# Weight blocks 129 columns apart, and four starting offsets for the chunks, in a float32r kernel of two layers

## The chip, the cores and the metric

The kernel runs on one core of a Trainium2 chip. The metric is the device time of one execution in microseconds (us). The engines are called as in the profile: PE is TensorE's matmul side and PEld its weight loads, DVE is VectorE, ACT is ScalarE, POOL is GpSimd, and SP issues most of the DMAs.

## The reference, cut to what matters

Two transformer layers follow each other on 256 tokens of width 1024 (the first adds 16 meta tokens, so that part of it works on 272 columns). Nearly all of the arithmetic is a chain of products of activations with weight matrices:

```python
# first layer
h = h + 0.5 * swiglu(rms_norm(h, ffn1_norm), ffn1_w_in, ffn1_w_out)   # 1024 -> 2 x 2816 -> 1024
h = h + token_mixer(rms_norm(h, mix_norm), ...)                       # w_in, two attentions, two branches, w_out
h = h + 0.5 * swiglu(rms_norm(h, ffn2_norm), ffn2_w_in, ffn2_w_out)
# second layer
h = h + head_group_mixer(rmsnorm(h), ...)                             # convolution and retention
h = h + memory_cross_attention(rmsnorm(h), rmsnorm(mem), ...)
h = h + jnp.square(jax.nn.relu(rmsnorm(h) @ up_w)) @ down_w           # 1024 -> 4096 -> 1024
```

All inputs and outputs are float32.

## The kernel before

Activations are held with the features on the 128 partitions and the tokens along the free axis: `XH[:, k]` is feature block k of the normed input for 256 tokens (272 in the first feed-forward network and the key and value projections). Each float32 operand is split into a float32r high part and a float32r low part that holds the rest, and each product is made of three float32r matmuls (`mm3`, lines 512 to 515): high weights by high activations, high weights by low activations, low weights by high activations. In each of them the weight block, 128 by 128, is the stationary operand (a weight load of its own, shown as PEld) and the activations are the moving operand, 256 or 272 columns. In `products_t` (lines 1005 to 1007) it is the other way round: 512 weight columns move past a stationary block of activations.

The weights come from HBM as chunks of at most 2048 columns, in the order of use (`_plan`). A chunk is a row of blocks, and nearly all blocks are 128 columns wide; 8 blocks of the forget gate have 8 columns, and the blocks for `products_t` have 512. `_Weights` handles a chunk in three steps, and each kind of tile has three buffers:

- `load` brings the chunk to a tile `raw` (SP's queue);
- `_high` (line 319, ACT) copies up to 1024 columns of `raw` to `hi`, which rounds them to float32r;
- `piece` (line 335, DVE) writes `lo = raw - hi` for the same columns.

`get(key)` gives PE the columns of `hi` and `lo` that hold one block. `core.step` sets the order: it first splits what the step's matmuls need, lets PE run, and splits for later steps, up to 4096 columns ahead, between the pieces of the work that empties PSUM. Everything is in the order in which the program writes it; no scheduler moves anything.

Where things lie in a partition matters for the change. A `hi` or `lo` tile is 2112 columns (8448 bytes, 33 times 256) wide, and its blocks begin 16 columns in:

```python
t = self.pool.tile([P, CH + LINE], F32R, tag=tag, bufs=3, name=f"{tag}{c}")   # CH = 2048, LINE = 64
return t[:, SHIFT : SHIFT + CH]                                               # SHIFT = 16
```

By the addresses that the program is given, every 128-column weight block of the kernel before begins 192 bytes past a multiple of 256, and every moving activation operand 128 bytes past one. The feature blocks of XH and XL lie 320 columns apart (1280 bytes). Some projections read their 256 moving columns as two runs of 128 that lie 144 columns (576 bytes) apart (`xq`); the second run then begins 192 bytes past a multiple of 256, as the weights do.

Three further places serve as measures below. The eight blocks of 8 columns (`fa`) begin 32 bytes further each. In the attention heads three float32 transposes (lines 688 to 690) load a block of the softmax result as weights; the third begins 144 columns (576 bytes) into the tile in the first eight heads and 145 columns (580 bytes) in the other eight. And line 814 (`factor`) is a DVE product whose operands are two runs of 128 columns.

Of the kernel before, what the change touches and what calls it, by code (L numbers as in the profile page):

```python
# [10 lines left out]
F32 = mybir.dt.float32  # L11
F32R = mybir.dt.float32r
I32 = mybir.dt.int32
AF = mybir.ActivationFunctionType
ALU = mybir.AluOpType
AX = mybir.AxisListType

P = 128
# [5 lines left out]
TP = 288  # L24
XP = 320
LINE = 64
SHIFT = 16
DFF = 2816
MF = DFF // P
DFF2 = 4096  # L30
# [4 lines left out]
CH = 2048  # L35
# [239 lines left out]
class _Weights:  # L275
# [2 lines left out]

    def __init__(self, nc, pool, ws):
        self.nc, self.pool, self.ws = nc, pool, ws  # L280
        _, self.where, self.start, self.ends, self.total = _plan()
        self.raw, self.hi, self.lo = {}, {}, {}
        self.loaded = 0
        self.c, self.o = 0, 0
        self.begun = []
        self.done = 0
        self.used = 0
        self.free = 0
        self.beside = None
# [16 lines left out]
    def _part(self, tag, c):  # L306


        t = self.pool.tile([P, CH + LINE], F32R, tag=tag, bufs=3, name=f"{tag}{c}")
        return t[:, SHIFT : SHIFT + CH]  # L310

    def _high(self, n):
        c, a = self.c, self.o
        at, size = self.start[c]
        if a == 0:
            self.hi[c] = self._part("hi", c)
            self.lo[c] = self._part("lo", c)
        b = min(a + n, size)
        self.nc.scalar.activation(self.hi[c][:, a:b], self.raw[c][:, a:b], AF.Copy)  # L319
        self.begun.append((c, a, b))  # L320
        self.c, self.o = (c + 1, 0) if b == size else (c, b)

    def piece(self, to, n=1024):


        if to is None or self.done >= to or self.done >= self.total:
            return False
        while sum(self.start[self.free]) <= self.used:
            self.free += 1
        while len(self.begun) < 2 and self.c < min(len(self.start), self.free + 3):  # L330
            self._high(n)
        c, a, b = self.begun.pop(0)
        if self.beside:
            self.beside((b - a) / 1024)
        self.nc.vector.tensor_tensor(self.lo[c][:, a:b], self.raw[c][:, a:b], self.hi[c][:, a:b].bitcast(F32),  # L335
                                     op=ALU.subtract)
        self.done = self.start[c][0] + b
        if b == self.start[c][1]:
            self.load()
        return True  # L340
# [16 lines left out]
    def get(self, key):  # L357
        c, off, n = self.where[key]
        self.used = max(self.used, self.start[c][0] + off + n)
        return self.hi[c][:, off : off + n], self.lo[c][:, off : off + n]  # L360


# [1243 lines left out]
```

## Time and profile before

| what | value |
|---|---|
| median of 2 runs | 983.17 us (982.59 to 983.75) |
| the profiled execution | 983.64 us |
| its span, from the first to the last instruction | 981.6 us |
| PE busy | 965.1 us (98% of the span), 7667 matmuls |
| DVE busy | 675.4 us (69%) |
| ACT busy | 537.5 us (55%) |
| DMA moved | 169.05 MB, 172 GB/s on average |

Matmuls are pipelined: one takes some 0.28 us from start to end, and the next starts before it has ended, so a PE that is "busy" may still be waiting in part. What a matmul costs is read from the distance between the starts of two matmuls, called the spacing here. In a table of stretches, the spacing is the stretch plus 0.28 us (the matmuls that had begun before it are counted) divided by the count of matmuls.

### The profile page before, as it was taken

How to read it: one execution, taken by the hardware profiler on the slowest of the kernel's cores; microseconds unless marked ns; L12 is line 12 of the kernel's file. 1: busy time of each engine (PE TensorE's matmuls, PEld its weight loads, DVE VectorE, ACT ScalarE, POOL GpSimd, SP SyncE). 2: the span in 40 equal slices, each digit the busy share in tenths (PEclk: the TensorE clock that was granted, in tenths of full speed). 3: DMA queues.
4: the chain of work that ended last, by engine and by line, in shares of the span. 5: the costliest groups of instructions: out<-in, count | busy, mean ns of one | idle time of the engine just before them, and what ended most of it. 6: DMA issues, size and time to landing. Idle time of an engine off the chain costs nothing.

```text
span 981.6 us, 18397 instructions
## 1 busy us (share of the span) xinstructions
PE 965.1 (98%) x7667; PEld 935.2 (95%) x7667; DVE 675.4 (69%) x1232; ACT 537.5 (55%) x927; POOL 9.9 (1%) x15
## 2 busy tenths in 40 slices
PE   7999999999999999999999999999999999999996
PEld 7999999999989899999999999889899999999996
DVE  5686656657875758677666657999976677675552
ACT  6545444456574656666454447556484566554441
POOL 0000000020000000000000000000000000000000
PEclk9999999999999999999999999999999999999999
DMA  8674526554523225554544656443544256555431
GB/s 298 191 264 172 173 92 233 191 185 138 173 94 123 96 99 214 215 215 173 194 166 157 209 191 235 168 155 138 202 159 155 86 182 221 199 194 194 173 128 43
DMA packets 31363, 169.05 MB, mean 172 GB/s; under 512 B 5144, under 2 KB 8864, under 8 KB 14640
## 3 DMA queue, kind: packets, MB, share of 16 engines
q1 hardware_dynamic: 30928, 167.34, 48.3%
q8 instruction: 60, 0.98, 0.4%
q10 hardware_dynamic: 288, 0.52, 0.1%
q14 instruction: 23, 0.19, 0.1%
q0 software_dynamic: 64, 0.01, 0.0%
HBM read 166.79 MB, written 1.07 MB: 171 GB/s over the span
## 4 chain that ended last, share of the span: by engine, by line
PE 75%; ACT 1%; DVE 1%; issue 0%; DVEq 0%
PE ps L513 14%; PE ps L515 14%; PE ps L514 14%; PE po L515 7%; PE po L514 7%; PE po L513 7%; PE ps L660 1%; PE ps L1007 1%; PE ps L1006 1%; PE ps L1005 1%; PE po L702 1%; PE ps L1308 1%; PE ps L1174 0%; PE po L1346 0%; PE po L716 0%; PE ps L766 0%
## 5 line engine op out<-in xcount | busy, mean ns | idle before, releaser
L335 DVE TENSOR_TENSOR lo<-raw,hi 128x1024 fp32r<-128x1024 f32 (+2 forms) x334 | 373.4, 1130 | 47.5 <-ACT hi L319 45.0
L319 ACT ACTIVATE hi<-raw 128x1024 fp32r<-128x1024 f32 (+2 forms) x334 | 321.8, 978 | 137.2 <-issue 43.8
L513 PE MATMUL ps<-XH,hi 128*128 128x256 f32 (+2 forms) x976 | 284.0, 291 | 5.7 <-ACT hi L319 4.3
L515 PE MATMUL ps<-XH,lo 128*128 128x256 f32 (+2 forms) x976 | 277.4, 284 | 0.8 <-DVE lo L335 0.8
L514 PE MATMUL ps<-XL,hi 128*128 128x256 f32 (+2 forms) x976 | 277.6, 284 | 0.0
L513 PEld LDWEIGHTS ps<-XH,hi 128*128 128x128 f32 (+1 forms) x976 | 184.4, 189 | 8.2 <-ACT hi L319 4.3
L514 PEld LDWEIGHTS ps<-XL,hi 128*128 128x128 f32 (+1 forms) x976 | 186.0, 191 | 1.8 <-DVE XL L527 0.5
L515 PEld LDWEIGHTS ps<-XH,lo 128*128 128x128 f32 (+1 forms) x976 | 184.3, 189 | 1.4 <-DVE lo L335 1.0
L513 PE MATMUL po<-XH,hi 128*128 128x256 f32 (+1 forms) x456 | 130.2, 285 | 0.2 <-DVE br L1071 0.2
L515 PE MATMUL po<-XH,lo 128*128 128x256 f32 (+1 forms) x456 | 129.0, 283 | 0.4 <-DVE lo L335 0.4
L514 PE MATMUL po<-XL,hi 128*128 128x256 f32 (+1 forms) x456 | 128.7, 282 | 0.0
L514 PEld LDWEIGHTS po<-XL,hi 128*128 128x128 f32 x456 | 86.7, 190 | 0.1
L515 PEld LDWEIGHTS po<-XH,lo 128*128 128x128 f32 x456 | 85.8, 188 | 0.6 <-DVE lo L335 0.6
L513 PEld LDWEIGHTS po<-XH,hi 128*128 128x128 f32 x456 | 85.7, 188 | 0.6 <-DVE br L1071 0.5
L624 ACT ACTIVATE s<-gr 128x272 f32<-128x272 f32 (+1 forms) x44 | 18.7, 426 | 108.5 <-DVE gr L622 108.5
L513 PE MATMUL ps<-AHf,hi 128*128 128x272 f32 (+1 forms) x220 | 62.4, 284 | 0.0
L514 PE MATMUL ps<-ALf,hi 128*128 128x272 f32 (+1 forms) x220 | 62.4, 284 | 0.0
L515 PE MATMUL ps<-AHf,lo 128*128 128x272 f32 (+1 forms) x220 | 62.4, 284 | 0.0
L1045 DVE SCALAR_TENSOR_TENSOR cv<-U,par,cv 128x256 f32<-128x256 f32 x120 | 50.1, 479 | 0.2 <-ACT cv L1078 0.2
L622 DVE TENSOR_TENSOR gr<-ps,r 128x272 f32<-128x272 f32 (+1 forms) x28 | 12.1, 434 | 48.4 <-PE ps L515 42.1
L513 PE MATMUL ps<-AHm,hi 128*128 128x256 f32 x160 | 45.0, 281 | 0.0
L514 PE MATMUL ps<-ALm,hi 128*128 128x256 f32 x160 | 45.0, 281 | 0.0
(385 smaller groups left out, 1827.8 us busy)
## 6 DMA issues: line engine op xcount, KB each, us to landing
raw<-in_ws_dram SPq DMA_DIRECT2D x128, 1024.0 KB, 4.8
raw<-in_ws_dram SPq DMA_DIRECT2D x32, 704.0 KB, 4.2
raw<-in_ws_dram SPq DMA_DIRECT2D x3, 512.0 KB, 5.6
dec<-in_dec_dram SPq DMA_DIRECT2D x1, 1536.0 KB, 6.4
BM<-drow SPq DMA_DIRECT2D x2, 512.0 KB, 5.7
memraw<-in_mt_dram SPq DMA_DIRECT2D x1, 1024.0 KB, 7.0
hA<-in_xt_dram SPq DMA_DIRECT2D x3, 273.0 KB, 6.0
raw<-in_ws_dram SPq DMA_DIRECT2D x3, 256.0 KB, 6.7
```

The costliest lines, as they stand in the source:

```text
L319: self.nc.scalar.activation(self.hi[c][:, a:b], self.raw[c][:, a:b], AF.Copy)
L335: self.nc.vector.tensor_tensor(self.lo[c][:, a:b], self.raw[c][:, a:b], self.hi[c][:, a:b].bitcast(F32), op=ALU.subtract)
L513: T.matmul(o, w[0], x[0], start=start, stop=False)
L514: T.matmul(o, w[0], x[1], start=False, stop=False)
L515: T.matmul(o, w[1], x[0], start=False, stop=stop)
L622: V.tensor_tensor(gr, g[:, :n], r[0][:, :n], op=ALU.mult)
L624: S.activation(s, gr, AF.Silu)
L660: T.matmul(ps[:, at : at + n], lhs, rhs, start=True, stop=True)
L702: T.matmul(o, st["v"](h, 0), pt[:, :SEQ], start=t % 2 == 0, stop=False)
L1005: T.matmul(ps[i], xh[:, t], wh, start=k == 0, stop=False)
L1006: T.matmul(ps[i], xl[:, t], wh, start=False, stop=False)
L1045: V.scalar_tensor_tensor(cv[:, m], U[:, m, j : j + SEQ], prm("cw", m * 31 + j), cv[:, m], op0=ALU.mult, op1=ALU.add)
```

## The change

In the split parts `hi` and `lo`, blocks of 128 columns now begin 129 columns (516 bytes) apart, with one unused column behind each. `raw` stays as it was. `_high` and `piece` therefore write (and `piece` reads `hi`) as runs of 128 with a step of 129: a piece of 1024 columns has the shape 8 x 128. Chunks with blocks of other widths (the one with the 8-column blocks, and those of `products_t`) keep blocks that touch. The fixed `SHIFT` of 16 columns gives way to a start of `16 * (c % 4)` columns for chunk c, and a tile is 16 columns wider (8512 bytes, 33.25 times 256), so the three buffers themselves begin 64 bytes further each, modulo 256. The six tiles take 384 bytes more in all, and what is allocated behind them moves by that: the moving operands there (AHf, AHm, OFH, OS, OXH, CH and their low parts, and YL) begin at a multiple of 256 bytes instead of 128 past one; XH, XL, YH, MH and ML stay.

No instruction is added, removed or moved on any engine. The start of a weight block now takes each of the 64 possible places of a 4-byte word in 256 bytes, with 86 to 142 matmuls each.

```diff
-SHIFT = 16
+GAP = 1
...
-        _, self.where, self.start, self.ends, self.total = _plan()
+        self.chunks, self.where, self.start, self.ends, self.total = _plan()
...
-        t = self.pool.tile([P, CH + LINE], F32R, tag=tag, bufs=3, name=f"{tag}{c}")
-        return t[:, SHIFT : SHIFT + CH]
+        t = self.pool.tile([P, CH + 16 + LINE], F32R, tag=tag, bufs=3, name=f"{tag}{c}")
+        at = 16 * (c % 4)
+        return t[:, at : at + CH + 16]
+
+    def _gap(self, c):
+        return GAP if all(b[4] == P for b in self.chunks[c]) else 0
+
+    def _blocks(self, t, c, a, b):
+
+        w = P + self._gap(c)
+        i, j = a // P, b // P
+        if w == P or a % P or b % P:
+            return t[:, a:b]
+        return t[:, i * w : j * w].rearrange("p (i w) -> p i w", w=w)[:, :, :P]
+
+    def _plain(self, t, c, a, b):
+        if not self._gap(c):
+            return t[:, a:b]
+        return t[:, a:b].rearrange("p (i w) -> p i w", w=P)
...
-        self.nc.scalar.activation(self.hi[c][:, a:b], self.raw[c][:, a:b], AF.Copy)
+        self.nc.scalar.activation(self._blocks(self.hi[c], c, a, b), self._plain(self.raw[c], c, a, b), AF.Copy)
...
-        self.nc.vector.tensor_tensor(self.lo[c][:, a:b], self.raw[c][:, a:b], self.hi[c][:, a:b].bitcast(F32),
-                                     op=ALU.subtract)
+        self.nc.vector.tensor_tensor(self._blocks(self.lo[c], c, a, b), self._plain(self.raw[c], c, a, b),
+                                     self._blocks(self.hi[c], c, a, b).bitcast(F32), op=ALU.subtract)
...
         self.used = max(self.used, self.start[c][0] + off + n)
+        off += off // P * self._gap(c)
         return self.hi[c][:, off : off + n], self.lo[c][:, off : off + n]
```

## Rows read from the trace of the kernel before

**Rows 1.** The page, part 1: busy time and share of each engine.
```profile
PE 965.1 (98%) x7667; PEld 935.2 (95%) x7667; DVE 675.4 (69%) x1232; ACT 537.5 (55%) x927; POOL 9.9 (1%) x15
```

**Rows 2.** Stretches, PE alone: us, busy (matmuls), granted clock, DMA share, GB/s.
```profile
35.00:205.00 170.00, 170.00 (x1381) 1.00 0.56 189
...
362.00:410.00 48.00, 48.00 (x426) 1.00 0.60 216
415.00:588.00 173.00, 173.00 (x1471) 1.00 0.53 184
602.00:613.00 11.00, 11.00 (x100) 1.00 0.35 111
...
723.00:737.00 14.00, 14.00 (x126) 1.00 0.59 204
775.00:798.00 23.00, 23.00 (x205) 1.00 0.48 162
805.00:965.00 160.00, 160.00 (x1361) 1.00 0.48 172
```

**Rows 3.** PE in order of time, 410.5 to 412.0 us: start, duration, instruction.
```profile
410.52 0.28 PE L515 MATMUL ps<-XH,lo 128*128 128x256 f32 x1
410.64 0.28 PE L513 MATMUL ps<-XH,hi 128*128 128x256 f32 x1
...
410.86 0.28 PE L515 MATMUL ps<-XH,lo 128*128 128x256 f32 x1
410.98 0.59 PE L562 MATMUL ps<-acc,c 128*128 128x256 f32 x2
411.22 0.47 PE L513 MATMUL po<-XH,hi 128*128 128x256 f32 x1
411.53 0.28 PE L514 MATMUL po<-XL,hi 128*128 128x256 f32 x1
411.65 0.28 PE L515 MATMUL po<-XH,lo 128*128 128x256 f32 x1
411.76 0.28 PE L513 MATMUL po<-XH,hi 128*128 128x256 f32 x1
```

**Rows 4.** PE in order of time, the forget gate's blocks of 8 columns.
```profile
237.32 0.29 PE L514 MATMUL ps<-XL,hi 128*8 128x272 f32 x1
...
237.82 0.28 PE L515 MATMUL ps<-XH,lo 128*8 128x272 f32 x1
237.94 0.29 PE L513 MATMUL ps<-XH,hi 128*8 128x272 f32 x1
...
238.31 0.29 PE L513 MATMUL ps<-XH,hi 128*8 128x272 f32 x1
238.44 0.29 PE L514 MATMUL ps<-XL,hi 128*8 128x272 f32 x1
...
240.05 0.29 PE L515 MATMUL ps<-XH,lo 128*8 128x272 f32 x1
```

**Rows 5.** PE in order of time, moving operand of two runs 576 bytes apart.
```profile
316.20 0.28 PE L513 MATMUL ps<-XH,hi 128*128 128x256 f32 x1
...
316.92 0.28 PE L513 MATMUL ps<-XH,hi 128*128 128x256 f32 x1
```

**Rows 6.** PE in order of time, transposes of a head of the second attention.
```profile
348.75 0.27 PE L688 MATMUL ps<-cst,p 128*128 128x128 f32 x1
348.86 0.27 PE L689 MATMUL ps<-cst,p 128*128 128x128 f32 x1
348.97 0.27 PE L690 MATMUL ps<-cst,p 128*128 128x128 f32 x1
```

**Rows 7.** All instructions of line 690: duration in ns, shortest, median, longest.
```profile
L690 PEld LDWEIGHTS ps<-cst,p x16: 138/140/144, 271.5 to 348.9; 128*128 128x128 f32 x16
```

**Rows 8.** Groups by line and shape on DVE: busy us, mean ns, idle before.
```profile
L335 DVE TENSOR_TENSOR lo<-raw,hi 128x1024 fp32r<-128x1024 f32 x291 | 352.6, 1219 | 47.2 <-ACT hi L319 44.7
...
L1414 DVE TENSOR_TENSOR a<-ps,t 128x256 f32<-128x256 f32 x20 | 8.4, 422 | 0.9 <-ACT t L1412 0.8
...
L814 DVE TENSOR_TENSOR hB<-ps,r 128x256 f32<-128x256 f32 x8 | 3.4, 424 | 7.1 <-PE ps L515 7.1
```

**Rows 9.** Groups by line and shape in 615 to 704 us, DVE.
```profile
L335 DVE TENSOR_TENSOR lo<-raw,hi 128x1024 fp32r<-128x1024 f32 x26 | 31.7, 1219 | 0.0
```

**Rows 10.** Stretch 615 to 704 us: us, then PE, PEld, DVE, ACT, POOL busy, clock, DMA.
```profile
615.00:704.00 89.00, 88.85 (x581) 78.61 (x581) 87.27 (x168) 48.19 (x74) 0.00 (x0) 1.00 0.43 155
```

**Rows 11.** Waits: who waited for whom, us in total, times, longest us.
```profile
DVE lo L335 <- ACT hi L319: 45.0, 34, 2.5
```

## Prediction

> **What bounds the kernel now.** I read the shares first: PE is busy for 965.1 us of the 981.6, its weight loads for 935.2, DVE for 69% and ACT for 55% [rows 1]. So PE sets the time, and the question is what one matmul costs. That is the spacing of starts, and the table of stretches gives it, at a granted clock of 1.00 throughout, which is the 2.4 GHz level [rows 2]. In the first feed-forward network, 272 columns wide: (170 + 0.28) / 1381 = 123.3 ns. In the second, 256 columns wide: 173.28 / 1471 = 117.8 ns, and in the last one 160.28 / 1361 = 117.8 ns. But in four other stretches with the same shape of matmul it is 48.28 / 426 = 113.3 ns, 112.8, 113.3 and 113.6 ns [rows 2]. Columns alone would take 256 / 2.4 = 106.7 ns and 272 / 2.4 = 113.3 ns. So 6.7 to 11 ns go astray in each matmul, and for one shape there are two levels of loss.
>
> The rows in order of time show where a level changes. Up to 410.86 us the matmuls start 0.11 us apart, then a statistic of two float32 passes (line 562) comes between, and behind it they start 0.12 us apart and stay so [rows 3]; the next such stretch holds for 173 us. DVE's work and the DMAs change all the time meanwhile, the spacing does not: it is a rhythm into which matmul and weight load fall, and which lasts until something interrupts it. In the kernel before, every weight block and every moving operand stand in the same relation modulo 256 bytes, so nothing in the addresses can push the rhythm out again. The change gives each block another relation.
>
> **The change part by part.** *Split pieces on DVE.* The same 334 instructions, with runs of 128 instead of one run. A DVE product of 256 columns takes 422 ns in one run and 424 ns in two [rows 8]; seven more runs in a piece of 1024 are then 14 ns on 1219. Between 615 and 704 us DVE is busy for 87.27 of 89 us, and there it can set the pace [rows 10]; 26 such pieces fall there [rows 9]: 26 x 14 ns = 0.4 us. Elsewhere DVE's idle time covers it. I take 0. *Copies on ACT.* No pair of rows compares one run with eight. DVE waited 45 us for these copies, in 34 waits [rows 11], but the splits run ahead of PE, and at 14 ns each as on DVE it would be under 0.5 us on 34 of them; I take 0 as well.
>
> *Weight loads from an address that is no multiple of 64 bytes.* The trace has such loads: of the 16 loads at line 690 eight begin 4 bytes further than the other eight. All take 138 to 144 ns [rows 7], and in a head with the odd start its load lies in the spacing before it, 0.11 us, as for the even one ahead of it [rows 6]. So the odd start costs a load nothing by itself; 0.
>
> The Trainium skill's page "SBUF — State Buffer" (section "Specifications (TRN2)") speaks against the change: it gives lines of 16 bytes and a penalty for each crossing to a new one. A block that begins off such a line touches 33 of them instead of 32. By that rule loads get longer; the loads of line 690, at 138 to 144 ns with either start, do not show it.
>
> *The spacing.* This is the term that counts. Two bounds come from the rows for 256 columns, 113.3 and 117.8 ns. If the relation changes with each block, neither rhythm should hold, and I take the mean of the two: of the matmuls in the listed stretches 2832 run at 117.8 and 857 at 113.3 or near [rows 2]; drawn evenly, 1844 would run at either, so (2832 - 1844) x 4.5 ns = 4.4 us are saved. For 272 columns the nearest row to a start that changes from block to block is the forget gate's: its blocks begin 32 bytes further each, and from 237.32 to 240.05 us there are 22 spacings, 2.73 / 22 = 124.1 ns, uneven, between 0.12 and 0.13 us [rows 4]. That is 0.8 ns over 123.3: 1381 x 0.8 = 1.1 us lost. The load there is of 8 columns only, and yet the spacing is no smaller; so much of the loss belongs to the moving operand, whose addresses in this first network stay for two thirds of the matmuls (XH and XL) and move by 128 bytes for the rest. Matmuls with 512 moving columns and two-run operands I leave as they are.
>
> Sum, against the profiled execution of 983.64 us (2.0 us beyond its span, 0.5 us over the median): 983.6 - 4.4 + 1.1 + 0 = 980.3, say 980 us. Its own range is 976 to 989: from the gain taken twice to no gain and the 857 at the upper level too (857 x 4.5 = 3.9 us).
>
> **Rivals.** *The good rhythm everywhere.* If an interrupted rhythm always finds the 113.3 ns level, 2832 x 4.5 = 12.7 us go. The lowest spacing in the forget gate's rows is 0.12 us [rows 4]; at 120 ns, 272 columns would save 1381 x 3.3 = 4.6 us. Time 983.6 - 17.3 = 966 us. For it: the same shape runs at 113.3 for 48 us on end. Against it: nothing in the trace says which relation leads there. A stronger form drops the loss altogether: the transposes, with a full weight load each, start 0.11 us apart, 109 ns at the least [rows 6], and 272 columns would take 6.7 ns more: 2832 x 8.8 + 857 x 4.3 + 1381 x 7.6 = 39 us, and 945 us.
>
> *Slower: a shifted relation is the dear one.* Where the moving operand consists of two runs, its second run begins 64 bytes further modulo 256 against the weights, and the spacing is 0.72 / 6 = 120 ns [rows 5], above both levels of the plain operand, every time. If that comes from the relation and not from the second run, three quarters of the chunks now stand in another relation than the one the kernel had, and 256 columns go to 120 ns: 2832 x 2.2 + 857 x 6.7 = 12.0 us; 272 columns to the upper end of the uneven rows, 0.13 us or 126.7 ns: 1381 x 3.4 = 4.7 us; the some 1500 matmuls of short groups, at 2.5 ns, 3.7 us more. Time 983.6 + 20.4 = 1004 us. It decides as soon as the mean over all relations lies above 117 ns for 256 columns.
>
> *The addresses do not matter.* Then the order of instructions, which is unchanged, brings the same rhythms after the same interruptions, and the time is 984 us; a slightly different length of a DVE piece may flip a long stretch, worth 1471 x 4.5 = 6.6 us down. For it: the forget gate's 8-column loads leave the spacing where it is [rows 4], and DVE and DMA never move it.
>
> The Trainium skill, "TensorE: Matmul & The Clock Gate" (section "Step-by-step: what each phase is for"), says that the two operands come through independent read ports, so that a load takes nothing from a running matmul. By that rule this rival holds and the change gives 984 us; that the spacing has two levels for one shape, the trace shows without saying which port is at fault.
>
> **How the numbers follow.** Chances: the forecast (980) 0.30; addresses without effect (984) 0.22; the good rhythm everywhere (966) 0.18, and the loss gone (945) 0.07; the shifted relation dear (1004) 0.23. Over 2% faster means under 963.5 us, and over 2% slower above 1002.8 us; that is about what a measurement of this kernel can tell from no change. Faster: the 0.07, and somewhat over half of the 0.18, since 966 stands close to the bound: 0.17. Slower: three quarters of the 0.23, also close to its bound: 0.17. Same: 0.66. The range of 8 in 10 leaves out the 945 and the upper part of the slow case: 961 to 1006 us.
>
> **What would show it.** The spacing in the same stretches. Right: for 256 columns a mean near 115.5 ns, uneven from block to block, and no stretch of 100 us at one level; 124 ns for 272 columns; pieces of 1024 columns at 1219 to 1235 ns on DVE; PEld durations as before. The dear relation: 120 ns or more, in some chunks (c modulo 4, or the place in the chunk) and not in others. Without effect: 113.3 and 117.8 ns again, constant over long stretches. I am wrong in kind if the spacing stays and another engine ends the chain: DVE or ACT pieces well above 1250 ns, with PE waiting for `lo` or `hi`.

## The result, and the profile after

The changed kernel takes 993.58 us (two runs, 993.40 and 993.75) against 983.17 us: a ratio of 1.0106, with a 95% interval of 1.0062 to 1.0149. That is a loss of 10 us, small but certain, where a gain of 3 us was forecast. The profiled execution spans 991.4 us against 981.6, 9.8 us more.

What did not move comes first. The page's part 1 answers to [rows 1]; the busy time of PE and of its weight loads (PEld) grows by 10.1 us each, and no other engine's by as much as 1 us:

```profile
PE 975.2 (98%) x7667; PEld 945.3 (95%) x7667; DVE 676.1 (68%) x1232; ACT 537.7 (54%) x927; POOL 9.9 (1%) x15
```

The groups by line and shape show the pieces that are now written as 8 runs of 128 (DVE's is line 352, ACT's line 336):

```profile
L352 DVE TENSOR_TENSOR lo<-raw,hi 128x1024 fp32r<-128x1024 f32 x291 | 352.7, 1220 | 49.4 <-ACT hi L336 44.8 <-PE po L533 2.0
...
L336 ACT ACTIVATE hi<-raw 128x1024 fp32r<-128x1024 f32 x291 | 303.2, 1051 | 137.1 <-issue 45.6 <-PE ps L532 42.3 <-PE po L532 29.1
```

The DVE piece went from 1219 ns [rows 8] to 1220. ACT's group in the kernel before had the same 291 pieces at a mean of 1050 ns:

```profile
L319 ACT ACTIVATE hi<-raw 128x1024 fp32r<-128x1024 f32 x291 | 303.0, 1050 | 132.7 <-issue 43.8 <-PE ps L514 36.7 <-PE po L514 29.0
```

And DVE waits for ACT's copies as long as it did [rows 11]:

```profile
DVE lo L352 <- ACT hi L336: 45.1, 33, 2.6
```

So the loss is in the spacing of PE's matmuls. The table of stretches, PE alone, for the same stages as [rows 2] (columns as there: us, busy with the count of matmuls, granted clock, DMA share, GB/s):

```profile
35.00:208.00 173.00, 173.00 (x1379) 1.00 0.56 187
362.00:415.00 53.00, 53.00 (x451) 1.00 0.57 208
420.00:593.00 173.00, 173.00 (x1464) 1.00 0.53 183
...
608.00:619.00 11.00, 11.00 (x95) 1.00 0.37 118
729.00:744.00 15.00, 15.00 (x129) 1.00 0.53 184
783.00:807.00 24.00, 24.00 (x205) 1.00 0.47 171
...
812.00:975.00 163.00, 163.00 (x1379) 1.00 0.48 168
```

The first network: 173.28 / 1379 = 125.7 ns for 272 columns, where it was 123.3. All stretches with 256 columns now have one level: 53.28 / 451 = 118.1 ns, 173.28 / 1464 = 118.4, 118.7, 118.4, 118.4 and 163.28 / 1379 = 118.4 ns. There had been two, 113.3 and 117.8. The granted clock is 1.00 in each row of both tables, the 2.4 GHz level, so the clock has no part in it. With these the span can be accounted for: 1379 x 2.4 ns = 3.3 us in the first network; 451 x 4.8 = 2.2 us and about 2.2 us more in the three short stretches, which left 113 ns; (1464 + 1379) x 0.6 = 1.7 us in the two long ones that were at 117.8 already. That is 9.4 of the 9.8 us.

In order of time the spacing is uneven now. PE in the second network, from 450.50 us on; the rows behind the statistic in [rows 3] answer to it:

```profile
450.50 0.28 PE L533 MATMUL ps<-XH,lo 128*128 128x256 f32 x1
450.62 0.28 PE L531 MATMUL ps<-XH,hi 128*128 128x256 f32 x1
450.74 0.28 PE L532 MATMUL ps<-XL,hi 128*128 128x256 f32 x1
450.85 0.29 PE L533 MATMUL ps<-XH,lo 128*128 128x256 f32 x1
450.98 0.28 PE L531 MATMUL ps<-XH,hi 128*128 128x256 f32 x1
451.09 0.28 PE L532 MATMUL ps<-XL,hi 128*128 128x256 f32 x1
```

The steps are 0.12, 0.12, 0.11, 0.13 and 0.11 us. So the rhythms are gone, as the prediction said; what comes instead is not their mean, it lies above both. That the addresses do it is for the experiments to show.

### The profile page after: what moved, and what is told of

It reads as the page before. It is cut to its first block, busy times and chain, and to the rows that moved or that the text cites. A ratio compares the mean times of both kernels' runs of the same rounds, so it can differ in the third digit from the quotient of the medians.

```text
span 991.4 us, 18397 instructions
## 1 busy us (share of the span) xinstructions
PE 975.2 (98%) x7667; PEld 945.3 (95%) x7667; DVE 676.1 (68%) x1232; ACT 537.7 (54%) x927; POOL 9.9 (1%) x15
## 4 chain that ended last, share of the span: by engine, by line
PE 96%; DVE 1%; DMA 1%; ACT 1%; SPq 1%; issue 0%; DVEq 0%
PE ps L533 19%; PE ps L531 18%; PE ps L532 18%; PE po L533 10%; PE po L532 10%; PE po L531 10%; PE ps L678 1%; PE ps L1025 1%; PE ps L1024 1%; PE ps L1023 1%; PE po L720 1%; DMA raw<-in_ws_dram 1%; PE ps L1326 1%; PE ps L1192 0%; PE po L1364 0%; PE po L734 0%
## 5 line engine op out<-in xcount | busy, mean ns | idle before, releaser
L533 PE MATMUL ps<-AHm,lo 128*128 128x256 f32 x160 | 44.9, 281 | 0.0
```

The lines of the kernel that those rows point to most:

```text
L533: T.matmul(o, w[1], x[0], start=False, stop=stop)
```

## The experiments

The theory after this reading: the spacing depends on where a weight block starts against its moving operand, modulo 256 bytes. Call the start of the block less the start of the operand, modulo 256, the relation. In the kernel before it is 64 bytes for every product with split weights; the change lets it take every multiple of 4 bytes. The rivals: the odd starts off a 16-byte or 64-byte line cost something themselves; or the steps of 129 columns do; or the spacing of a stretch is set by the interruption alone, and the change merely had bad luck. The expectations name them by letters: A, a relation that changes from block to block gives the loss; A2, a rhythm only needs consecutive loads in the same relation, whichever it is; B, a start off a 16-byte line costs by itself; C, the moved chunk starts and operand tiles do it; D, only the relation of 64 bytes is a good one. Spacings below are worked out from stretches as above, and those of single chunks from the starts of the first matmuls of two chunks, divided by the 48 matmuls of a chunk.

### The change taken apart

**gap1_fixed** keeps the 129 columns and drops the moving start (edit against the changed kernel; the tile is 34 times 256 bytes, so that nothing behind it moves):

```diff
-        t = self.pool.tile([P, CH + 16 + LINE], F32R, ...)
-        at = 16 * (c % 4)
+        t = self.pool.tile([P, CH + 2 * LINE], F32R, ...)
+        at = 16
...
```

> Blocks 129 columns apart as in the change, but every chunk starts at 16 columns and a tile is 2176 columns wide, so that the buffers and all other tiles lie as before modulo 256. Theory A (a relation of weights and moving operand that changes from block to block keeps PE from falling into a rhythm): about 993 us, 118.4 ns for 256 columns and 125.6 ns for 272, uneven, as after the change. Theory B (a weight start off a 16-byte line costs by itself): 993 us too. Theory C (the moved chunk starts and moved operand tiles are to blame): 983 us, 113.3 and 117.8 ns in long stretches.

Measured: 995.59 us, ratio 1.0120 (1.0103 to 1.0137). The gap alone does the whole harm: 118.7 ns in the second network and 125.4 ns in the first.

**nogap_rot** drops the gap (`GAP = 0`) and keeps the start of `16 * (c % 4)`.

> No gap (blocks touch), but chunk starts of 16 * (c % 4) columns, tiles of 2128 columns and all other tiles moved as in the change. Theory A: the relation changes only between chunks and between hi and lo, always by multiples of 64 bytes; a rhythm can hold inside a chunk, 980 to 987 us. Theory B: 983 us, all starts lie on 16-byte lines. Theory C: about 993 us.

Measured: 990.33 us, 1.0071 (1.0054 to 1.0088); 117.5 ns (160.28 / 1364) and 125.8 ns (170.28 / 1354). Every block starts on a line of 64 bytes here and the kernel is still 7 us slower. The odd start is not needed for the loss. None of the three expectations had this time.

**gap4_fixed** is gap1_fixed with blocks 132 columns apart (`GAP = 4`), so that each block starts on a multiple of 16 bytes.

> Blocks 132 columns (528 bytes) apart, so that each starts on a 16-byte line but 16 bytes further than the last against the 64-byte grid; chunk starts and all other tiles as before modulo 256. Theory A: the relation still changes with each block, 989 to 994 us and uneven spacings. Theory B: 983 us with the two levels of before. Theory C: 983 us.

Measured: 990.46 us, 1.0074 (1.0059 to 1.0089). Its stretches:

```profile
35.00:205.00 170.00, 170.00 (x1361) 1.00 0.56 189
...
420.00:580.00 160.00, 160.00 (x1360) 1.00 0.54 185
```

170.28 / 1361 = 125.1 ns for 272 columns, 160.28 / 1360 = 117.9 ns for 256. Each block starts on a multiple of 16 bytes, and 7 of the 10 us of loss are there.

### A constant other relation

**shift17**, **shift20** and **shift48** are the kernel before with one number changed, so that all blocks have one relation, of 68, 80 and 192 bytes:

```diff
-SHIFT = 16
+SHIFT = 17
```

> The kernel before with all chunks starting at 17 columns instead of 16: every weight block starts 4 bytes off a 16-byte line, and all of them in the same way. Theory A: the relation is constant, a rhythm forms again: constant spacings over long stretches, 976 to 990 us (which level each stretch gets is open). Theory B: 993 us or more, since each load is off a line. Theory C: 983 us.

Measured: 991.17 us, 1.0078 (1.0063 to 1.0093).

```profile
35.00:205.00 170.00, 170.00 (x1373) 1.00 0.57 190
362.00:405.00 43.00, 43.00 (x366) 1.00 0.55 196
420.00:580.00 160.00, 160.00 (x1355) 1.00 0.54 187
```

124.0 ns for 272 columns, and 118.3 ns in both stretches of 256. Nothing rotates here, and the 113.3 ns of [rows 2] are gone nevertheless: four bytes off are enough. The time lies between what A and B had asked for.

> The kernel before with all chunks at 20 columns: starts on a 16-byte line but 16 bytes off the 64-byte grid, the same for all blocks. Theory D (and a 64-byte grid): one constant rhythm, no stretch at 113.3 ns, 989 to 993 us as with 17 columns. Theory B (16-byte lines): 983 us with the two levels of before. Theory A2 alone: 976 to 987 us.

Measured: 997.16 us, 1.0150 (1.0135 to 1.0166), the slowest of all: 118.6 to 118.9 ns, and 126.6 ns for 272 columns. A start on a multiple of 16 bytes is worse here than the odd one of shift17, and no theory had asked for this time.

> The weights of before, all 32 columns further, so that every weight block starts 192 bytes behind its moving tile modulo 256 instead of 64, with nothing else changed. If the relation of the two starts sets the spacing, every stretch shows what the chunks with this relation showed: 117.8 ns for 256 columns in all stretches and none at 113.3, 126.6 ns for 272 columns; against before 1205 x 4.5 ns and 1838 x 3.2 ns, some 11 us, so about 994 us. If a constant relation is as good as any other as long as nothing rotates, 983 us with stretches at 113.3.

Measured: 992.14 us, 1.0092 (1.0077 to 1.0107).

```profile
35.00:205.00 170.00, 170.00 (x1345) 1.00 0.55 184
...
420.00:580.00 160.00, 160.00 (x1361) 1.00 0.54 185
```

126.6 and 117.8 ns: the table that the relation theory had asked for, to 0.1 ns. The time is 2 us better than expected. Some 1 us of it is the operands of two runs, which the sum had left out: 576 matmuls, which fell from about 120 ns [rows 5] to about 118 here. As these operands still consist of two runs, the 120 ns came at least in part from the relation.

**hilo64** gives only `lo` another relation, 128 bytes, and leaves `hi` at 64:

```diff
-        return t[:, SHIFT : SHIFT + CH]
+        at = SHIFT if tag == "hi" else SHIFT + 16
+        return t[:, at : at + CH]
```

> The kernel before, with lo starting 64 bytes further than hi modulo 256 and nothing else changed: every third load has another relation. Theory A2: the rhythm is lost as in the run without a gap (there hi and lo lay 192 bytes apart), 989 to 992 us and uneven spacings of 117.5 and 125 ns. Theory D: two of three matmuls keep the good relation, 983 to 987 us.

Measured: 995.44 us, 1.0130 (1.0115 to 1.0145); 118.2 ns (160.28 / 1356) and 126.6 ns (170.28 / 1345). Two matmuls in three have the old relation and gain nothing by it: a third one between them with another relation spoils it, and 272 columns get as dear as in the worst constant case, not the 124.4 ns that the mean over the three would be. Both expectations were too low.

### One relation per chunk

**chunk_rot** has no gap, a tile of 34 times 256 bytes and the start of `16 * (c % 4)`: the relation is constant within a chunk and goes 0, 64, 128, 192 from chunk to chunk.

> Blocks touch, tiles of 2176 columns (all buffers and other tiles as before modulo 256), and chunk c starts at 16 * (c % 4) columns, so that the relation of weights and moving operand is one of four within a chunk, the same for hi and lo, and changes at chunk bounds. Theory A2 (a rhythm needs consecutive loads in the same relation): 980 to 987 us, constant spacings inside each chunk. Theory D (only the relation of the kernel before, 64 bytes past the moving operand modulo 256, is a good one): chunks with c % 4 = 1 keep 113.3 or 117.8 ns, the other three quarters are at 118.3 or more: 988 to 992 us.

Measured: 994.00 us, 1.0113 (1.0096 to 1.0130), the loss of the change within 1 us, with no odd start and no gap, and 2 us beyond the upper of the two expectations. PE in order of time, the first matmul of chunks 68 to 72 (second network, 256 columns):

```profile
428.28 0.28 PE L531 MATMUL ps<-XH,hi 128*128 128x256 f32 x1
...
434.04 0.28 PE L531 MATMUL ps<-XH,hi 128*128 128x256 f32 x1
...
439.69 0.27 PE L531 MATMUL po<-XH,hi 128*128 128x256 f32 x1
...
445.38 0.28 PE L531 MATMUL po<-XH,hi 128*128 128x256 f32 x1
...
451.04 0.28 PE L531 MATMUL ps<-XH,hi 128*128 128x256 f32 x1
```

Relation 0: 5.76 / 48 = 120.0 ns; 64: 5.65 / 48 = 117.7; 128: 5.69 / 48 = 118.5; 192: 5.66 / 48 = 117.9. The same in the first network, chunks 4 to 8 (272 columns):

```profile
37.24 0.28 PE L531 MATMUL ps<-XH,hi 128*128 128x272 f32 x1
...
43.25 0.29 PE L531 MATMUL po<-XH,hi 128*128 128x272 f32 x1
...
49.17 0.29 PE L531 MATMUL ps<-XH,hi 128*128 128x272 f32 x1
...
55.25 0.29 PE L531 MATMUL ps<-XH,hi 128*128 128x272 f32 x1
...
61.33 0.29 PE L531 MATMUL ps<-XH,hi 128*128 128x272 f32 x1
```

Relation 0: 6.01 / 48 = 125.2 ns; 64: 5.92 / 48 = 123.3; 128: 6.08 / 48 = 126.7; 192: 126.7. The means over the four are 118.5 and 125.5 ns. The change showed 118.4 and 125.7.

**gap16** is gap1_fixed with blocks 144 columns apart (`GAP = 16` and a larger tile): the relation moves by 64 bytes from block to block.

> The two split parts with their blocks 144 columns apart, so that the relation of the weight's start to the moving tile's moves by 64 bytes from block to block and every block starts on a 64-byte line; chunk starts as in before. If only the relation modulo 256 bytes counts, a stretch shows the mean of the four relations, 118.4 ns for 256 columns and 125.5 for 272, as the change does without its odd starts: 990 to 995 us. If the odd 4-byte starts have a part in the change's loss, this one lies clearly below the change, 983 to 987 us.

Measured: 992.58 us, 1.0095 (1.0078 to 1.0112).

```profile
35.00:205.00 170.00, 170.00 (x1358) 1.00 0.56 188
...
420.00:580.00 160.00, 160.00 (x1354) 1.00 0.54 185
```

125.4 and 118.4 ns: the mean of the four relations also when they change every three matmuls, and on lines of 64 bytes. The odd starts of the change are not needed for its loss. Whether they add to it these runs don't settle: gap1_fixed, with odd starts, is 3 us slower than gap16, but shift17, with them, is 6 us faster than shift20 without.

**move128** moves not the weights but the tiles allocated late, among them AHf and AHm, by 128 bytes (a pad of 32 columns ahead of the weight tiles, `SHIFT = 48`). Products of XH and XL keep the relation 64, those of AHf and AHm get 192.

> The weights as before modulo 256, but everything allocated behind the weight tiles moved by 128 bytes (AHf, AHm, OFH, OS, OXH, CH and their low parts, YL), as the change does; XH, XL, YH, MH and ML stay. Theory A2: 983 us, the relation is constant in each product. Theory D: the products of those operands (second half of each feed-forward network, branches, w_out_2, xo) lose the stretch at 113.3 ns or move to about 118.3, the products of XH keep their levels: 984 to 988 us.

Measured: 983.41 us, 1.0008 (0.9998 to 1.0017): no difference, but by a sum of two opposite ones.

```profile
35.00:140.00 105.00, 105.00 (x854) 1.00 0.56 185
150.00:205.00 55.00, 55.00 (x437) 1.00 0.60 205
...
455.00:525.00 70.00, 70.00 (x620) 1.00 0.47 167
535.00:585.00 50.00, 50.00 (x427) 1.00 0.59 202
```

In the first network the products of XH stay at 105.28 / 854 = 123.3 ns, those of AHf go to 55.28 / 437 = 126.5; so it is the relation that counts, and not the weight's own place. In the second, AHm's products take 50.28 / 427 = 117.8 ns; but XH's, at 117.8 in the kernel before, run at 70.28 / 620 = 113.4. Their relation is the old one. So the relation 64 allows two rhythms, and something that stands before the stretch picks one.

The trace shows more of this than the run was made for. Ahead of the statistic at 413.37 us, the same one as in [rows 3], XH's products run at the upper level here; these two rows are 42 matmuls apart, 4.94 / 42 = 117.6 ns:

```profile
408.07 0.28 PE L514 MATMUL ps<-XH,hi 128*128 128x256 f32 x1
...
413.01 0.28 PE L514 MATMUL ps<-XH,hi 128*128 128x256 f32 x1
```

Behind it they run at 113.4. In the kernel before it was the other way round, 113.3 ahead and 117.8 behind, with the same relation of 64 bytes on both sides in both kernels. So the interruption does not lead to one level; at this place it was followed by the other one than it found.

### What picks the rhythm

**kick** is the kernel before, with two of its more than 160 chunks at the relation 192. Chunk 66 is the first behind the statistic of [rows 3], chunk 133 stands where a statistic interrupts the last network:

```diff
-        return t[:, SHIFT : SHIFT + CH]
+        at = 48 if c in (66, 133) else SHIFT
+        return t[:, at : at + CH]
```

> The kernel before, with chunks 66 and 133 alone starting 32 columns further (relation 192 bytes); all other chunks have the relation of before, 64 bytes. Where a chunk with the relation 192 was followed by one with 64 in an earlier run, the rhythm of 113.3 ns followed. If that is a law, the long stretches from 416 us and from 806 us fall into 113.3 ns: (1391 + 1358) x 4.5 ns less, some 970 us. If the rhythm after an interruption is a matter of the moment alone, they keep 117.8 and the time is 983 us; a mixture lies between.

Measured: 970.31 us, ratio 0.9873 (0.9857 to 0.9890): faster than both kernels.

```profile
420.00:580.00 160.00, 160.00 (x1413) 1.00 0.56 191
```

The second network now takes 160.28 / 1413 = 113.4 ns where it took 117.8 [rows 2], and the last one, less a wait of 0.45 us, 151.83 / 1336 = 113.6 ns:

```profile
808.00:960.00 152.00, 151.55 (x1336) 1.00 0.48 171
```

The place where it changes, PE in order of time from the first matmul of chunk 67:

```profile
416.30 0.28 PE L514 MATMUL po<-XH,hi 128*128 128x256 f32 x1
...
416.66 0.28 PE L514 MATMUL ps<-XH,hi 128*128 128x256 f32 x1
...
417.00 0.28 PE L514 MATMUL po<-XH,hi 128*128 128x256 f32 x1
```

From 416.30 to 416.66 us three steps take 0.36 us; from 416.66 to 417.00 three take 0.34, that is 113 ns each. The level holds for the rest of the network, as the row of the stretch shows.

**kick0** does the same with chunks 67 and 134 and the relation 128 (`at = 32 if c in (67, 134)`).

> The kernel before, with chunks 67 and 134 alone starting 16 columns further (relation 128 bytes). The same question as the run with chunks 66 and 133, by another relation and one chunk later: 970 us where any change back to the relation of 64 bytes brings the rhythm of 113.3 ns, 983 us where it does not.

Measured: 970.89 us, 0.9873 (0.9859 to 0.9888). The second network at 160.28 / 1412 = 113.5 ns, and the last network, from 808 to 960 us, at 152.28 / 1343 = 113.4, where it was 117.8:

```profile
420.00:580.00 160.00, 160.00 (x1412) 1.00 0.56 193
808.00:960.00 152.00, 152.00 (x1343) 1.00 0.49 173
```

**kick_r0** is kick with the relation 0 in the two chunks (`at = 0 if c in (66, 133)`).

> The two-chunk run (chunks 66 and 133) with the relation 0 for these two chunks instead of 192. If any change back to 64 bytes brings the rhythm of 113.3 ns, 970 us. If it depends on where one comes from, and the relation 0 leads to 117.8 as in the first chunk run, the stretch from 417 us stays at 117.8, and the one from 806 us, which begins at 113.3 ahead of its statistic or not as before, too: 983 us.

Measured: 983.18 us, 1.0001 (0.9991 to 1.0011), the time of the kernel before.

```profile
420.00:580.00 160.00, 160.00 (x1361) 1.00 0.55 187
808.00:960.00 152.00, 152.00 (x1293) 1.00 0.51 181
```

117.8 ns in both. So a change of relation by itself does nothing: in these three runs one comes from 128 or 192 into the low rhythm, and from 0 into the high one.

**chunk_rev** is chunk_rot the other way round (`at = 16 * (-c % 4)`): 0, 192, 128, 64.

> The chunk run with its order turned round: the relation goes 0, 192, 128, 64 bytes from chunk to chunk instead of 0, 64, 128, 192, so that 64 is now reached from 128 instead of from 0. If what stands before decides the rhythm within the relation 64, its chunks of 256 columns show 113.3 to 114 ns (they were at 117.8 after 0), the others keep 119.9, 117.8 and 118.6: the mean goes from 118.6 to 117.5, 4591 x 1.0 = 4.6 us less than the first chunk run: 989 us. If the order does not matter: 994 us. Chunks of 272 columns keep 125.4, 126.6, 126.6 and 123.5 either way.

Measured: 985.82 us, 1.0032 (1.0019 to 1.0045), 8 us below chunk_rot with the same starts in another order. The first matmul of chunks 68 to 72:

```profile
427.27 0.28 PE L531 MATMUL ps<-XH,hi 128*128 128x256 f32 x1
...
433.03 0.28 PE L531 MATMUL ps<-XH,hi 128*128 128x256 f32 x1
...
438.48 0.28 PE L531 MATMUL po<-XH,hi 128*128 128x256 f32 x1
...
444.17 0.28 PE L531 MATMUL po<-XH,hi 128*128 128x256 f32 x1
...
449.62 0.28 PE L531 MATMUL ps<-XH,hi 128*128 128x256 f32 x1
```

Relation 0: 120.0 ns; 192: 5.45 / 48 = 113.5; 128: 118.5; 64: 113.5. It gained more than the expectation, because 192 has a low rhythm as well, which is reached from 0. Counted are the chunks with 256 columns whose matmuls run without another one among them. Of those with the relation 192, 18 of 21 stayed below 115 ns here, and none of 20 in chunk_rot, where 192 follows 128. For the relation 64 it is 18 of 20 here, after 128, and none of 21 in chunk_rot, after 0. So what stood before decides, but the relation before is not all of it. The two of the 20 at 117.8 ns, chunks 67 and 135, came after 128 too, shortly behind a statistic; and in chunk_rot some blocks of 64 that came after 0, those of chunk 65 at the start of the second network, ran at 113.3. The relations 0 and 128 showed one level each in the middle of the networks of both runs, 119.7 to 120.0 and 118.4 to 118.6 ns a chunk.

## Why the prediction was wrong

**What bounds the kernel** was right. PE alone grew, the spacing is the whole of the loss, DVE and ACT moved by under 1 us, and the DMA share of the stretches moved by at most 0.06. The loss, 1.1%, is also clear of noise, where the prediction had held about 2% to be what can be told from no change.

**DVE 0, ACT 0, the odd start of a load 0**: right. 1219 became 1220 ns, 1050 became 1051, and the costliest groups of the page have the weight loads at the same length, here one of them, first before, then after:

```profile
L515 PEld LDWEIGHTS po<-XH,lo 128*128 128x128 f32 x456 | 85.8, 188 | 0.6 <-DVE lo L335 0.6
```

```profile
L533 PEld LDWEIGHTS po<-XH,lo 128*128 128x128 f32 x456 | 85.9, 188 | 0.6 <-DVE lo L352 0.6
```

The Trainium skill's rule of 16-byte lines ("SBUF — State Buffer", "Specifications (TRN2)") would have had longer loads, and no loss for gap4_fixed, which keeps the lines: the loads are not longer, and that kernel loses 7 us.

**The step that failed is the term for 256 columns: "If the relation changes with each block, neither rhythm should hold, and I take the mean of the two."** The first half came true, the second did not follow. 113.3 and 117.8 ns are two states of one relation, 64 bytes; the change leads to other relations, and those have prices of their own. The four multiples of 64 average to 118.5 ns in chunk_rot, the changed kernel to 118.4. Instead of 4.4 us saved, the stretches of 256 columns lost 1.7 us where they had been at 117.8 and 4.4 us where they had been at 113.3. The bounds were taken from the only relation that the rows for 256 plain columns held, and the mean of two known states was used for a state that no row showed.

**The term for 272 columns** had the right sign and the wrong size: 0.8 ns forecast from the 8-column blocks [rows 4], 2.4 ns measured. Those blocks move by 32 bytes only from one to the next, with a load of 8 columns; chunk_rot gives the four prices, 123.3, 125.2, 126.7 and 126.7 ns. The relation of the kernel before was the cheapest of them, so a rotation over the four had to lose on these columns.

**The rivals.** "A shifted relation is the dear one" was the right mechanism with its point of decision: it was to hold as soon as the mean over all relations lay above 117 ns, and that mean is 118.4. Its price was too high, since 120 ns for 256 columns is paid at the relation 0 alone, and 126.7 ns for 272 at only two of the four multiples of 64: 1004 us forecast, 993.6 measured. "The good rhythm everywhere" (966 us) did not come with this change, but it exists: the prediction had said that nothing in the trace told which relation leads there, and kick gets to 970 us by it. "The loss gone" and "the addresses do not matter" fell; shift17, one number changed, costs 8 us. The rule of independent ports (the Trainium skill, "TensorE: Matmul & The Clock Gate", "Step-by-step: what each phase is for"), which spoke for the latter, does not account for these runs: start addresses alone move the spacing of 256 columns between 113.4 and 120 ns.

**What is open.** The runs show that the relation sets the spacing, not by what mechanism: none shows which of the two reads gives way, nor why the relation 0 leads into the high rhythm at 64 and into the low one at 192. The statistic at 411 us was followed by the high rhythm in the kernel before and by the low one in move128; why stays open.

## What to carry to other kernels

Where one engine is busy for 98% and its instructions are all alike, measure the distance of their starts per stretch, and treat two levels for one shape as a gain to be had: here two of more than 160 chunks, stored 128 bytes further, brought 13 us, while the change that touched every chunk lost 10. Before operands are rotated to break a bad pattern, give each relation a constant run of its own (one number changed per run): rotation over four relations gave about their mean in chunk_rot and gap16, and loses where the present one is the cheapest. The order counts too: chunk_rev, the same four the other way round, was 8 us faster. A mean of two observed states is no estimate for a state that was not observed.

## What the runs showed of the hardware that was not expected

- In this kernel, with a float32r block of 128 x 128 as weight and a load before each matmul, the spacing depends on the weight's start less the moving operand's start, modulo 256 bytes. At 256 columns: 120.0 ns at 0, 113.4 or 117.8 at 64, 118.5 at 128, 113.5 or 117.8 at 192, 118.3 at 68 and 118.7 at 80. At 272 columns: 125.2, 123.3, 126.7 and 126.7 ns at 0, 64, 128 and 192, 124.0 at 68 and 126.6 at 80.
- The rhythm has a memory. After a change to the relation 64 it settles within four matmuls and then holds, for 160 us in kick; the level depends on what stood before, the relation there (kick, kick0, kick_r0) but not it alone (chunk_rev, move128).
- A weight block with another relation in every third matmul (hilo64) takes the low level from the two others as well: 118.2 ns for 256 columns and 126.6 for 272.
- Eight runs of 128 columns, 129 columns apart, in place of one run of 1024 cost DVE and ACT 1 ns: 1219 to 1220 and 1050 to 1051.
